# Two tokens side by side in place of four in the operands of the gate products

## The chip, the cores and the metric

The kernel runs on one core of a Trainium2 chip. The metric is the device time of one execution in microseconds (us). Before the change it is 4701.33 us, the median of 3 runs (4699.65 to 4709.9).

## What is computed

Two trunk layers on 256 context tokens and 512 latent tokens of width 1024. Each layer has a mixer (layer 0: RWKV-7 heads and a Fourier transform, layer 1: attention and a convolution) and then a PEER block, a feed-forward of 16384 small experts. The change is in PEER alone:

```python
q = (tc @ pq).reshape(PEER_CHUNK, PK_HEADS, 2, PK_HALF)
s1 = einsum("thd,hnd->thn", q[:, :, 0], sk1); s2 = einsum("thd,hnd->thn", q[:, :, 1], sk2)
v1, i1 = top_k(s1, 16);  v2, i2 = top_k(s2, 16)
score, ci = top_k(v1[..., :, None] + v2[..., None, :], 16)    # of 256 pairs
e1, e2 = i1[ci // 16], i2[ci % 16]                            # each 0 to 127
expert = e1 * 128 + e2;  gate = softmax(score)
act = gelu(einsum("thkd,td->thk", pu[expert], tc)) * gate
out = einsum("thk,thkd->td", act, pv[expert])
```

So each token has 8 heads x 16 = 128 slots, each with an expert (e1, e2) and a gate.

## The kernel before

PEER comes in two ways. For most tokens (tiles of 128: four tiles in layer 0, three in layer 1) it is computed densely: all 16384 experts are multiplied with all tokens, and the product is weighted with a gate that is zero for the experts that a token hasn't chosen. For the other tiles (two of the context in layer 0, one in layer 1) the experts' rows are gathered from DRAM, one slot at a time (`gather`): POOL issues an indirect DMA, DVE works on the 128 x 1024 row that came.

`peer` has two parts. In the first, `select` (DVE) forms e1, e2 and the gates of a tile, `dense_gates` makes of them the dense gates and writes them to DRAM (`gd`), and beside that the first NB blocks of 128 experts (60 in layer 0, 48 in layer 1) go through `up_part`: load a block of pu (SP), split it in a high and a low part (`whi` on ACT, line 378, `wlo` on DVE, line 381), 24 float32r matmuls (line 391), Gelu on ACT. In the second part the gates come back (`gt`), are multiplied with the activations, and the product with pv is summed (line 1287; for the fourth tile of layer 0 line 1316), with the remaining blocks' `up_part` in between. The gathers' steps are spread over both parts.

`dense_gates` works for a tile of 128 tokens in 32 groups of four tokens. Slots lie on the partitions: e1, e2 and the gate are transposed on PE to 128 slots x 128 tokens and written as fp16 to `ee` (gxe: e1, e2) and `gg` (gxg: the gate times 32768 as a high part and a rest). Then for each group:

- DVE, line 1106: `o` (tile o12) = one-hot codes of e1 and of e2: for each slot, 2 x 128 keys x 4 tokens, by comparison of the constant `iob` (0 to 127, each repeated for the tokens side by side) with the repeated e1 and e2.
- DVE, line 1108: `og` = the code of e1 times the gate's high part, and times its rest.
- PE, line 1114: for each token two matmuls 128 x 128 x 128 (high part, rest) into `gps`: the code of e2 is loaded as weights, `og` streams. The sum over the slots is the token's gate for each pair of e2 and e1.
- ACT, line 1116: two operations take `gps` to `gbig`, which goes to DRAM after 64 tokens.

GW is the number of tokens side by side, that is, the innermost extent of `o`, `og` and `iob`. With 4, the operands of one token's matmul are fp16 elements at a step of 4, 8 bytes.

The order of instructions on each engine is fixed when the program is built, by a scheduler; on the chip each engine goes through its queue in that order and waits on semaphores. `o` and `og` have four buffers each (OB), `gps` three.

Of the kernel before, what the change touches and what calls it, by code (L numbers as in the profile page):

```python
# [8 lines left out]
F32 = mybir.dt.float32  # L9
F32R = mybir.dt.float32r  # L10
BF16 = mybir.dt.bfloat16
F16 = mybir.dt.float16
# [3 lines left out]
OP = mybir.AluOpType  # L16
# [14 lines left out]
CQ = 3  # L31
FB = 2
GSC = 32768.0
GW = 4
GQ = 0
NO = 0
NK = 0
# [29 lines left out]
OB = 4  # L67
# [126 lines left out]
class Net:  # L194
# [26 lines left out]
    def setup(self, st):  # L221
# [22 lines left out]
        self.ka1 = ka  # L244
        self.iob = p.tile([128, 128, GW], F16, name="iob")
        nc.vector.tensor_copy(self.iob, self.k("iota")[:, :, None].to_broadcast([128, 128, GW]))
        self.io16 = p.tile([128, 16, 16], BF16, name="io16")
# [839 lines left out]
    def dense_gates(self, e1, e2, gate, gd, sp, gp, pp, pt):  # L1087

        nc = self.nc
        V = nc.vector  # L1090


        ee, gg = sp.tile([128, 2, 128], F16, name="gxe"), sp.tile([128, 2, 128], F16, name="gxg")
        for dst, x, sc in ((ee[:, 0], e1, 1.0), (ee[:, 1], e2, 1.0), (gg[:, 0], gate, GSC)):
            p = pt.tile([128, 128], F32, name="gtp")
            nc.tensor.transpose(p, x.rearrange("p a b -> p (a b)"), self.k("ident"))
            nc.scalar.mul(out=dst, in_=p, mul=sc)
        V.scalar_tensor_tensor(out=gg[:, 1], in0=p, scalar=GSC, in1=gg[:, 0], op0=OP.mult, op1=OP.subtract)
        W, H = GW, 64
        for h0 in range(0, 128, H):  # L1100
            gh = [gp.tile([128, 64, H], F32, name="gbig") for _ in range(2)]
            for t0 in range(h0, h0 + H, W):
                w = slice(t0, t0 + W)
                o = sp.tile([128, 2, 128, W], F16, name="o12", bufs=OB)
                og = sp.tile([128, 2, 128, W], F16, name="og", bufs=OB)
                V.tensor_tensor(out=o, in0=self.iob[:, None].to_broadcast([128, 2, 128, W]),  # L1106
                                in1=ee[:, :, None, w].to_broadcast([128, 2, 128, W]), op=OP.is_equal)
                V.tensor_tensor(out=og, in0=o[:, 0:1].to_broadcast([128, 2, 128, W]),  # L1108
                                in1=gg[:, :, None, w].to_broadcast([128, 2, 128, W]), op=OP.mult)
                for k0 in range(0, W, 4):  # L1110
                    p = pp.tile([128, 4, 128], F32, name="gps")
                    for j in range(4):
                        for i in range(2):
                            nc.tensor.matmul(p[:, j, :], o[:, 1, :, k0 + j], og[:, i, :, k0 + j], start=(i == 0), stop=(i == 1))  # L1114
                    for i, g in enumerate(gh):
                        nc.scalar.mul(out=g[:, :, t0 - h0 + k0:t0 - h0 + k0 + 4].rearrange("p e t -> p t e"), in_=p[:, :, i * 64:i * 64 + 64],  # L1116
                                      mul=1.0 / GSC)
            for i, g in enumerate(gh):
                nc.scalar.dma_start(gd[h0 // H, :, i * 64:i * 64 + 64, :], g)

# [500 lines left out]
```

## Time and profile before

| | |
|---|---|
| median of 3 runs | 4701.33 us (4699.65 to 4709.9) |
| the profiled execution | 4686.23 us |
| its span | 4684.4 us |
| PE, DVE, ACT, POOL busy | 91%, 76%, 37%, 34% of the span |
| PE's granted clock, mean | 0.95 |
| the gate products (line 1114) | 1792 loads and 1792 matmuls |
| the DVE operations before them (lines 1106, 1108) | 224 each |

The profile is of one execution. PE is the matmul engine, PEld its loading of weights, which can run beside a matmul; L1114 is line 1114 of the kernel before. A matmul's duration contains the time that it takes to run through the array, and matmuls overlap; what one costs in a row of them is the distance from start to start. A row of a timeline gives start, duration, engine, line, operation, output<-inputs, sizes and count. A row of windows gives a stretch, its length, then for each engine its busy time and number of instructions, then the granted clock of PE, the busy share of the DMA engines and GB/s.

### The profile page before, as it was taken

Reading aid. Unit: us, or ns where it says so; the run is one execution under the profiler, and the core shown is the slowest. Engines: PE = TensorE matmul, PEld = TensorE weight load, DVE = VectorE, ACT = ScalarE, POOL = GpSimd, SP = SyncE. Lnnn points to the kernel's source line nnn. Section 1 sums busy time; section 2 is a strip of 40 time slices with the busy share of each in tenths; the row PEclk is TensorE's granted clock in tenths of the full one; section 3 lists DMA queues with packets and bytes.
Section 4 is the critical chain, followed back from the end, with each engine's and each line's share of the span. In section 5 each row is a group of like instructions: output and inputs, shape, how many; then the busy total and the mean of one; then the engine's idle time right before and its main releaser. Section 6 shows DMA issues by size and latency. Waiting matters only on the chain. (4 is left out here: it accounts for less than half of the span.)

```text
span 4684.4 us, 69766 instructions
## 1 busy us (share of the span) xinstructions
PE 4278.9 (91%) x26113; PEld 3540.5 (76%) x26113; DVE 3552.1 (76%) x6647; ACT 1739.0 (37%) x2845; POOL 1577.4 (34%) x1146
## 2 busy tenths in 40 slices
PE   7998899985769999999999999879999989999998
PEld 5775567874647887877777888666789978888887
DVE  2776566689899887888788787695488877788885
ACT  3443123333224556222222222336436643333333
POOL 1332112214643120444444344383220024444440
PEclk9998898997889999999999999889999989999999
DMA  4444873335777767989888888410135589999994
GB/s 167 97 105 106 268 272 115 111 127 184 225 240 266 250 242 263 321 303 322 292 306 314 302 307 286 154 31 32 70 110 183 201 326 330 337 350 334 335 332 153
DMA packets 487278, 1061.99 MB, mean 227 GB/s; under 512 B 95094, under 2 KB 265846, under 8 KB 477206
## 3 DMA queue, kind: packets, MB, share of 16 engines
q1 hardware_dynamic: 371740, 594.02, 38.5%
q0 software_dynamic: 110592, 402.70, 24.6%
q10 hardware_dynamic: 4608, 60.82, 3.3%
q8 instruction: 205, 3.36, 0.3%
q14 instruction: 133, 1.09, 0.1%
HBM read 927.83 MB, written 129.56 MB: 226 GB/s over the span
## 5 line engine op out<-in xcount | busy, mean ns | idle before, releaser
L1128 POOL DMA_INDIRECT row<-in_l_pv_dram,gi x384 | 539.0, 1404 | 912.1 <-DVE rows L1142 778.1
L1128 POOL DMA_INDIRECT row<-in_l_pur_dram,gi x384 | 477.5, 1243 | 972.2 <-DVE ga L1133 511.7
L391 PE MATMUL pS<-h2hi,whi 128*128 128x512 f32 (+1 forms) x2048 | 754.6, 368 | 36.9 <-ACT a L1233 32.2
L391 PE MATMUL pS<-h2hi,wlo 128*128 128x512 f32 (+1 forms) x2048 | 752.7, 368 | 5.1 <-DVE wlo L381 5.1
L391 PE MATMUL pS<-h2lo,whi 128*128 128x512 f32 (+1 forms) x2048 | 751.8, 367 | 0.0
L1133 DVE CUSTOM_DVE_ANT_0 row<-row,rows 128x1024 f32<-128x1024 f32 x384 | 495.7, 1297 | 170.5 <-DMA row<-in_l_pur_dram,gi 168.1
L378 ACT CAST whi<-wraw 128x1024 fp32r<-128x1024 f32 x327 | 343.9, 1053 | 750.5 <-PE pS L391 571.6
L1142 DVE SCALAR_TENSOR_TENSOR rows<-row,ga,rows 128x1024 f32<-128x1024 f32 x381 | 488.2, 1281 | 158.5 <-DMA row<-in_l_pv_dram,gi 156.4
L1287 PE MATMUL acc<-vhi,ahi 128*128 128x512 f32 x1536 | 469.6, 392 | 11.3 <-ACT ahi L378 11.3
L1287 PE MATMUL acc<-vlo,ahi 128*128 128x512 f32 x1536 | 478.3, 391 | 0.0
L1287 PE MATMUL acc<-vhi,alo 128*128 128x512 f32 x1536 | 472.1, 391 | 3.5 <-DVE alo L381 3.5
L391 PEld LDWEIGHTS pS<-h2hi,whi 128*128 128x128 f32 x2048 | 390.3, 191 | 84.6 <-ACT a L1233 34.1
L391 PEld LDWEIGHTS pS<-h2hi,wlo 128*128 128x128 f32 x2048 | 389.3, 190 | 47.8 <-DVE wlo L381 6.8
L391 PEld LDWEIGHTS pS<-h2lo,whi 128*128 128x128 f32 x2048 | 390.5, 191 | 44.0
L381 DVE TENSOR_TENSOR wlo<-wraw,whi 128x1024 fp32r<-128x1024 f32 x266 | 325.6, 1224 | 85.6 <-ACT whi L378 84.8
L378 ACT CAST vhi<-vraw 128x1024 fp32r<-128x1024 f32 x256 | 265.0, 1050 | 215.3 <-PE acc L1287 107.7
L381 DVE TENSOR_TENSOR vlo<-vraw,vhi 128x1024 fp32r<-128x1024 f32 x256 | 309.8, 1221 | 40.1 <-ACT vhi L378 39.9
L1287 PEld LDWEIGHTS acc<-vhi,alo 128*128 128x128 f32 x1536 | 289.0, 188 | 66.3 <-DVE alo L381 5.1
L1287 PEld LDWEIGHTS acc<-vhi,ahi 128*128 128x128 f32 x1536 | 288.1, 189 | 65.9 <-ACT ahi L378 11.9
L1287 PEld LDWEIGHTS acc<-vlo,ahi 128*128 128x128 f32 x1536 | 289.3, 188 | 61.3
L378 ACT CAST ahi<-a32f 128x384 fp32r<-128x384 f32 (+1 forms) x148 | 83.3, 563 | 594.6 <-DVE a32f L1303 279.5
L1116 ACT ACTIVATE gbig<-gps 128x256 f32<-128x256 f32 x448 | 235.5, 661 | 156.8 <-PE gps L1114 144.4
(460 smaller groups left out, 8175.9 us busy)
## 6 DMA issues: line engine op xcount, KB each, us to landing
wraw<-in_l_pu_dram SPq DMA_DIRECT2D x256, 512.0 KB
vraw<-in_l_pv_dram SPq DMA_DIRECT2D x256, 512.0 KB
gd<-gbig ACTq DMA_DIRECT2D x28, 2048.0 KB
mw<-in_l_mod_w_dram SPq DMA_DIRECT2D x48, 1024.0 KB
gt<-gd SPq DMA_DIRECT2D x64, 512.0 KB
wraw<-in_l_pq_dram SPq DMA_DIRECT2D x48, 512.0 KB
gt<-gd SPq DMA_DIRECT2D x64, 384.0 KB
ab<-arb SPq DMA_DIRECT2D x24, 768.0 KB
```

The costliest lines, as they stand in the source:

```text
L378: e.copy(out=hi, in_=src)
L381: return (e_lo or nc.vector).tensor_tensor(out=lo, in0=src, in1=hi.bitcast(F32), op=OP.subtract)
L391: nc.tensor.matmul(ps, a[:, k, :], b[:, k, t0:t0 + n], start=s, stop=e)
L1116: nc.scalar.mul(out=g[:, :, t0 - h0 + k0:t0 - h0 + k0 + 4].rearrange("p e t -> p t e"), in_=p[:, :, i * 64:i * 64 + 64], mul=1.0 / GSC)
L1128: nc.gpsimd.indirect_dma_start(out=r, out_offset=None, in_=self.I[f"l{l}_{src}"], in_offset=bass.IndirectOffsetOnAxis(ap=idx[:, s:s + 1], ...
L1133: V.tensor_tensor_reduce(out=r, in0=r, in1=acc, scale=1.0, scalar=0.0, op0=OP.mult, op1=OP.add, accum_out=act[:, s:s + 1])
L1142: V.scalar_tensor_tensor(out=acc, in0=r, scalar=act[:, s:s + 1], in1=acc, op0=OP.mult, op1=OP.add)
L1287: nc.tensor.matmul(acc[t][h2], x[:, q], y[:, h2 * 512:(h2 + 1) * 512], start=s, stop=z)
```

## The change

GW becomes 2. `o` and `og` still hold four tokens, now as two pairs: the innermost extent is 2, and the pair's number lies outside the keys. In the same way `ee` and `gg` are held in pairs of tokens. So

- a matmul's operands, weights and stream, are fp16 elements at a step of 2, 4 bytes, in place of 4, 8 bytes;
- the two DVE operations have the same number, size and output; the operand that is repeated over the keys (`ee`, `gg`) is read in rows of 2 elements in place of 4;
- the three ACT operations and one DVE operation of a tile that fill `ee` and `gg` go in pairs of elements, and `iob` has 256 in place of 512 columns.

The program has the same instructions in the same order on every engine.

```diff
--- before.py
+++ after.py
@@ -31,7 +31,7 @@
 CQ = 3
 FB = 2
 GSC = 32768.0
-GW = 4
+GW = 2
 GQ = 0
 NO = 0
 NK = 0
@@ -1090,31 +1090,33 @@
         V = nc.vector
 
 
-        ee, gg = sp.tile([128, 2, 128], F16, name="gxe"), sp.tile([128, 2, 128], F16, name="gxg")
-        for dst, x, sc in ((ee[:, 0], e1, 1.0), (ee[:, 1], e2, 1.0), (gg[:, 0], gate, GSC)):
+        W, H = GW, 64
+        two = lambda x: x.rearrange("p (a b) -> p a b", b=W)
+        ee, gg = sp.tile([128, 64, 2, W], F16, name="gxe"), sp.tile([128, 64, 2, W], F16, name="gxg")
+        for dst, x, sc in ((ee[:, :, 0], e1, 1.0), (ee[:, :, 1], e2, 1.0), (gg[:, :, 0], gate, GSC)):
             p = pt.tile([128, 128], F32, name="gtp")
             nc.tensor.transpose(p, x.rearrange("p a b -> p (a b)"), self.k("ident"))
-            nc.scalar.mul(out=dst, in_=p, mul=sc)
-        V.scalar_tensor_tensor(out=gg[:, 1], in0=p, scalar=GSC, in1=gg[:, 0], op0=OP.mult, op1=OP.subtract)
-        W, H = GW, 64
+            nc.scalar.mul(out=dst, in_=two(p), mul=sc)
+        V.scalar_tensor_tensor(out=gg[:, :, 1], in0=two(p), scalar=GSC, in1=gg[:, :, 0], op0=OP.mult, op1=OP.subtract)
         for h0 in range(0, 128, H):
             gh = [gp.tile([128, 64, H], F32, name="gbig") for _ in range(2)]
-            for t0 in range(h0, h0 + H, W):
-                w = slice(t0, t0 + W)
-                o = sp.tile([128, 2, 128, W], F16, name="o12", bufs=OB)
-                og = sp.tile([128, 2, 128, W], F16, name="og", bufs=OB)
-                V.tensor_tensor(out=o, in0=self.iob[:, None].to_broadcast([128, 2, 128, W]),
-                                in1=ee[:, :, None, w].to_broadcast([128, 2, 128, W]), op=OP.is_equal)
-                V.tensor_tensor(out=og, in0=o[:, 0:1].to_broadcast([128, 2, 128, W]),
-                                in1=gg[:, :, None, w].to_broadcast([128, 2, 128, W]), op=OP.mult)
-                for k0 in range(0, W, 4):
-                    p = pp.tile([128, 4, 128], F32, name="gps")
-                    for j in range(4):
-                        for i in range(2):
-                            nc.tensor.matmul(p[:, j, :], o[:, 1, :, k0 + j], og[:, i, :, k0 + j], start=(i == 0), stop=(i == 1))
-                    for i, g in enumerate(gh):
-                        nc.scalar.mul(out=g[:, :, t0 - h0 + k0:t0 - h0 + k0 + 4].rearrange("p e t -> p t e"), in_=p[:, :, i * 64:i * 64 + 64],
-                                      mul=1.0 / GSC)
+            for t0 in range(h0, h0 + H, 4):
+
+                w = slice(t0 // W, t0 // W + 2)
+                o = sp.tile([128, 2, 2, 128, W], F16, name="o12", bufs=OB)
+                og = sp.tile([128, 2, 2, 128, W], F16, name="og", bufs=OB)
+                B4, B5 = [128, 4, 128, W], [128, 2, 2, 128, W]
+                V.tensor_tensor(out=o.rearrange("p a h e b -> p (a h) e b"), in0=self.iob[:, None].to_broadcast(B4),
+                                in1=ee[:, w].rearrange("p a h b -> p (a h) b")[:, :, None].to_broadcast(B4), op=OP.is_equal)
+                V.tensor_tensor(out=og, in0=o[:, :, 0:1].to_broadcast(B5), in1=gg[:, w, :, None].to_broadcast(B5), op=OP.mult)
+                p = pp.tile([128, 4, 128], F32, name="gps")
+                for j in range(4):
+                    a, b = divmod(j, W)
+                    for i in range(2):
+                        nc.tensor.matmul(p[:, j, :], o[:, a, 1, :, b], og[:, a, i, :, b], start=(i == 0), stop=(i == 1))
+                for i, g in enumerate(gh):
+                    nc.scalar.mul(out=g[:, :, t0 - h0:t0 - h0 + 4].rearrange("p e t -> p t e"), in_=p[:, :, i * 64:i * 64 + 64],
+                                  mul=1.0 / GSC)
             for i, g in enumerate(gh):
                 nc.scalar.dma_start(gd[h0 // H, :, i * 64:i * 64 + 64, :], g)
```

## Rows read from the trace of the kernel before

**Rows 1.** The profile's page, first part: busy time of the engines.
```profile
PE 4278.9 (91%) x26113; PEld 3540.5 (76%) x26113; DVE 3552.1 (76%) x6647; ACT 1739.0 (37%) x2845; POOL 1577.4 (34%) x1146
```

**Rows 2.** Windows: stretch, length, then PE, PEld, DVE, ACT, POOL, clock, DMA.
```profile
1484.00:1800.00 316.00, 316.00 (x1752) 265.20 (x1751) 268.11 (x508) 176.80 (x293) 57.54 (x41) 1.00 0.69 243
1800.00:1860.00 60.00, 52.00 (x344) 43.45 (x343) 42.06 (x66) 40.84 (x76) 0.00 (x0) 0.83 0.63 248
3520.00:3760.00 240.00, 238.09 (x1569) 229.49 (x1568) 201.03 (x447) 154.10 (x258) 0.00 (x0) 1.00 0.52 188
3760.00:3800.00 40.00, 35.56 (x234) 33.03 (x233) 29.71 (x47) 24.09 (x44) 9.54 (x8) 0.79 0.89 341
3900.00:4600.00 700.00, 698.09 (x3413) 620.00 (x3412) 560.13 (x692) 248.37 (x338) 302.82 (x220) 1.00 0.94 333
2000.00:3000.00 1000.00, 946.60 (x4093) 767.17 (x4092) 791.22 (x982) 267.18 (x360) 405.79 (x310) 0.99 0.86 295
```

**Rows 3.** Timeline of PE: float32r matmuls one behind the other, 512 and 256 columns.
```profile
1610.77 0.39 PE L391 MATMUL pS<-h2hi,whi 128*128 128x512 f32 x1
...
1614.19 0.39 PE L391 MATMUL pS<-h2hi,whi 128*128 128x512 f32 x1
...
1040.72 0.28 PE L391 MATMUL po<-hchi,whi 128*128 128x256 f32 x1
...
1041.90 0.28 PE L391 MATMUL po<-hclo,whi 128*128 128x256 f32 x1
```

**Rows 4.** Timeline of PE and PEld: a run of 24 gate pairs.
```profile
1607.44 2.73 PEld L1114 LDWEIGHTS <-o 128*128 128x128 f16 x24 [0.26 <-DVE rows L1142]
1607.45 3.02 PE L1114 MATMUL gps<-og,o 128*128 128x128 f16 x24
```

**Rows 5.** Groups by shape: busy us, mean ns of one, idle time before.
```profile
L1114 PE MATMUL gps<-og,o 128*128 128x128 f16 x1792 | 234.3, 296 | 10.8 <-ACT gbig L1116 6.2 <-DVE og L1108 3.0
...
L391 PEld LDWEIGHTS pS<-h2lo,whi 128*128 128x128 f32 x2048 | 390.5, 191 | 44.0
...
L1114 PEld LDWEIGHTS <-o 128*128 128x128 f16 x1792 | 194.1, 118 | 41.5 <-issue 21.7 <-PE gps L1114 8.7 <-DVE og L1108 2.9
...
L857 PEld LDWEIGHTS sm<-sv,M 32*32 32x32 f32 x576 | 34.0, 106 | 14.6 <-DVE sv L858 4.5 <-issue 2.1 <-DVE am L803 1.9
```

**Rows 6.** Windows, line 1114 alone: stretch, length, PE, PEld, clock, DMA.
```profile
1484.00:1800.00 316.00, 98.13 (x752) 81.37 (x753) 1.00 0.69 243
1800.00:1860.00 60.00, 35.26 (x274) 29.87 (x272) 0.83 0.63 248
3520.00:3760.00 240.00, 82.10 (x624) 67.11 (x624) 1.00 0.52 188
3760.00:3800.00 40.00, 18.85 (x144) 15.74 (x144) 0.79 0.89 341
```

**Rows 7.** Windows, line 391 alone, first main part.
```profile
1484.00:1800.00 316.00, 239.41 (x991) 182.78 (x989) 1.00 0.69 243
```

**Rows 8.** Groups of DVE by shape: busy us, mean ns; and L1077: minimum/median/maximum ns.
```profile
L1106 DVE TENSOR_TENSOR o<-iob,gxe 128x1024 f16<-128x1024 f16 x224 | 151.9, 687 | 54.0 <-PE gps L1114 52.3 <-issue 0.7 <-ACT gxe L1097 0.3
L1108 DVE TENSOR_TENSOR og<-o,gxg 128x1024 f16<-128x1024 f16 x224 | 148.1, 683 | 0.1
L381 DVE TENSOR_TENSOR wlo<-wraw,whi 128x1024 fp32r<-128x1024 f32 x266 | 325.6, 1224 | 85.6 <-ACT whi L378 84.8
...
L1077 DVE TENSOR_TENSOR teq<-taf,io x10: 1211/1220/2308, 1081.2 to 3726.4; 128x2048 bf16<-128x2048 bf16 x10
```

**Rows 9.** Waits from 1484 to 1800 us: us in total, times, longest.
```profile
POOL row L1128 <- DVE rows L1142: 152.8, 25, 9.0
...
ACT whi L378 <- PE pS L391: 43.5, 24, 3.9
...
DVE wlo L381 <- ACT whi L378: 22.6, 22, 2.6
DVE o L1106 <- PE gps L1114: 21.9, 29, 2.8
```

## The prediction, made before the run

> **What bounds the kernel now.** I began with the page's busy shares: PE is busy 91% of the span [rows 1]. A busy PE is not yet a full one, so I then read the two stretches in which the changed lines run, by windows. They lie in the first half of each PEER layer: 1484 to 1860 us and 3520 to 3800 us. In both, the main part comes first and a tail follows.
>
> In the main part of the first one (316 us) PE is busy for all of it, in that of the second for 238.1 of 240 us [rows 2]. Whether that is full is told by counting. A matmul of 512 columns in the neighbouring product (line 391) follows the last one after 0.228 us: 15 steps take 1614.19 - 1610.77 = 3.42 us [rows 3]. A gate matmul follows the last one after (3.02 - 0.296) / 23 = 0.118 us, in a run of 24 [rows 4]; the 0.296 us is the last one's own duration [rows 5]. In 316 us there are 991 of line 391 and 752 of the gate products [rows 6, 7]: 991 x 0.228 + 752 x 0.118 = 314.7 us. So PE does nothing else and hardly waits. What these 752 pairs (a load and a matmul each) cost is on the path in full. The same holds for the 624 pairs of the second main part.
>
> In the tails (274 and 144 pairs) it is otherwise: PE is busy 52.0 of 60 and 35.6 of 40 us, at a granted clock of 0.83 and 0.79 [rows 2]. For each four tokens DVE needs two operations of 0.685 us [rows 8], 1.37 us, against 8 x 0.118 = 0.94 us on PE. There DVE paces.
>
> DVE is the next engine in the main parts: 268.1 of 316 and 201.0 of 240 us [rows 2]. Its waits there are PE's doing: 21.9 us for the one-hot tile that PE still reads, and 22.6 us for ACT's whi, which itself waited 43.5 us for PE [rows 9]. Together 44.5 of its 47.9 us of idle time.
>
> **The change part by part.** No instruction comes, goes or moves on any engine; only how operands lie. So the sum has durations alone in it.
>
> 1. *The gate pairs on PE.* Load and matmul read fp16 elements 4 bytes apart in place of 8. No row has a 16-bit operand that lies closer, so the new time is bounded. From above: 0.118 us, no change. More than that I exclude, since each instruction reads the same elements from half the stretch. From below: the float32r matmuls of 256 columns, whose operands are contiguous, follow each other after 1.18 / 10 = 0.118 us [rows 3], those of 512 after 0.228; that is 0.43 ns a column, and 0.064 us at 128 columns, if the load hides behind the matmul as it does there.
>
> Does it hide here? A float32 load of 32 columns lasts 106 ns and one of 128 columns 191 ns [rows 5]: 78 ns fixed and 0.885 ns a column. The fp16 load lasts 118 ns, so some 40 ns of reading. In the run of 24, the loads stand end to end: 24 of 118 ns fill 2.73 us [rows 4, 5], one load for each step of a matmul. I read that as load and stream in turn: 40 ns, then 78 ns for 128 columns, 0.61 ns a column against the 0.43 above. Both are then slower than they need be. With the stream at 0.43 x 128 = 55 ns and the load as short as the shortest full one in these rows, 28 ns (0.885 x 32), a pair takes 83 ns. I take 84 ns: 34 ns less. It stands between the ends of 64 and 118, somewhat nearer to the first.
>
> The Trainium skill ("TensorE: Matmul & The Clock Gate", section "Back-to-back issue gap") gives some 81 ns a matmul for a steady stream of loads and matmuls at 128 columns; no run here shows it for 16 bits. An estimate by that figure is 37 ns x 1376 = 51 us of PE time in the main parts.
>
> On the path: 752 x 34 = 25.6 us and 624 x 34 = 21.2 us. PE's need falls to 290 and 219 us, DVE's stays at 268 and 201, 92% of each. The queues are served in order, so some of the idle time that DVE keeps will fall where PE needs its result; I count nine tenths, 42 us. In the tails 418 x 34 = 14 us of PE work lies beside DVE; I take 3 us of it, for the matmuls that DVE waits for there. Sum 45 us.
>
> 2. *The two DVE operations*, 224 of each, 1024 fp16 elements. The operand that is repeated now has rows of two elements in place of four. From below: 0.685 us as now. The bf16 comparison of 2048 elements in rows of 16 (line 1077) takes 1.22 us [rows 8], that is, 0.52 ns more for each further element, so rows of 4 and of 16 run at one rate. From above: the float32 operation of 1024 elements, 1.224 us [rows 8], if the chip can no longer take elements in pairs. I take the first: it is the same instruction, and two is still a pair. Nothing hides a loss here beyond DVE's idle time.
>
> 3. *The rest.* Each dense tile has three ACT operations and one of DVE on 128 x 128 that now write or read pairs: 28 instructions in all, beside PE's full work in the main parts. The constant iob has half the size. Nothing; without that cover it would be the difference of 28 short instructions.
>
> What follows a stretch is moved forward as a whole. The gathers' steps stand between the other instructions, and in the main part POOL's fetches wait for DVE (152.8 us) [rows 9], so they move with it. From 3900 to 4600 us PE is busy 698.1 of 700 us [rows 2], so layer 1's gain reaches the end; in layer 0 PE is at 946.6 of 1000 us after the stretch, with the same work behind the same work. The stretch would ask for DMA at 0.69 x 316 / 290 = 0.75 of the engines' time, while 3900 to 4600 runs at 0.94 with PE full [rows 2].
>
> The profiled execution took 4686.2 us for a span of 4684.4 us; the median of three runs is 4701.3, 15.1 us above it. 4686.2 - 45 = 4641, and with the 15.1 us 4656 us.
>
> **Rivals.**
>
> *The step does not matter (no change).* What makes 118 ns may be the turn-taking of load and matmul, not the reading: the load's 118 ns equals the spacing, and its first 78 ns are no reading at all by the fit above. Then the pair stays at 118 ns and the time at 4701 us. Against it: loads of float32 last 191 ns while their matmuls follow after 118, so a load's whole duration need not be waited for [rows 3, 5]. The Trainium skill ("Advanced Engine Details and Errata", section "Memory Cachelines") speaks for this rival: SBUF is read in lines of 16 bytes, and two accesses to one line are said to be enough for full speed. A step of 8 bytes already makes two. The trace leaves that open: the 0.61 ns a column speak against it, but they rest on my split of the 118 ns.
>
> *Only the load gains.* 40 to 28 ns, 12 x 1376 = 16.5 us on the path, 4685 us. For it: the fp16 load is longer than that of 32 columns by just this much. Against: the 23 ns that the stream has over the float32r slope would be unexplained.
>
> *DVE loses its pairs (slower).* Each of the 448 operations takes 1.224 us, 0.54 more. Layer 0: 256 x 0.54 = 138 us against 65.8 us of DVE idle time in main part and tail; layer 1: 192 x 0.54 = 104 against 49.3 us. DVE becomes the bound and the gain on PE is worth nothing: 72 + 54 = 126 us, 4827 us. It decides from about 0.94 us an operation, where the 65.8 us are used up (65.8 / 256 = 0.26 above 0.685). For it: rows this short stand nowhere in the trace. Against: rate independent of row length at 4 and 16.
>
> *A pair at the lower bound.* 64 ns, 54 x 1376 = 74 us of PE; PE's need is then 275 and 206 us, DVE 97% busy, so I count three quarters, 56 us, and 4 in the tails: 4641 us. This is the forecast's own lower half.
>
> **How the numbers follow.** Forecast, a pair between 64 and 95 ns: 0.63, time 4656 us, its own range 4636 to 4675. Load alone: 0.12. No change: 0.15. DVE slower: 0.10. What can be told from no change is 0.2%, 9.4 us. Faster: 0.63 + 0.12 = 0.75; within: 0.15; slower: 0.10. Downwards the full 74 us without loss would give 4627. The range goes from 4630 to 4706: it takes in no change with the scatter of the runs, and leaves out the slower rival and the last of the lower end.
>
> **What would show it.** In the profile after, the gate matmuls in a run should follow each other after about 84 ns, with loads of some 106 ns. L1106's and L1108's successors should still take 0.685 us; 1.2 us would be the slower rival. DVE's wait for the gate tiles (21.9 us) should shrink to a few us, and PE should show first idle time before gate loads, waiting for DVE. The two stretches should be 25 and 20 us shorter and all else as long as before. If pairs are at 84 ns and the stretches are not shorter, the step that failed is that PE bounds them; if pairs stay at 118, it is the reading.

## The result, and the profile after

The changed kernel takes 4617.97 us (median of 4 runs, 4613.54 to 4629.15) against 4700.49 us of the kernel before (4 runs, 4692.45 to 4709.9): ratio 0.9827 [0.9802, 0.9853], 82.5 us less. The same pair was run again later: 4616.06 against 4696.14 us, ratio 0.9821 [0.9799, 0.9842], 80.1 us less. Forecast were 4656 us and a range of 4630 to 4706. So the direction was right, and the gain of 45 us was a little over half of the real one; the time lies below the range.

The profiled execution of the changed kernel took 4615.68 us (span 4613.9 us). In the changed kernel the lines named before are shifted: L1106 is L1109, L1108 is L1111, L1114 is L1116, L1116 is L1118, L1128 is L1130, L1142 is L1144. So L1116 below is the gate matmul where a row is of the changed kernel, and the ACT operation behind it where a row is of the kernel before.

What answers to [rows 4]: a run of 24 gate pairs on PE, from the timeline of after (start us, length us, engine, line, operation, output<-inputs, sizes, count).

```profile
1490.33 1.38 PEld L1116 LDWEIGHTS <-o 128*128 128x128 f16 x24 [0.26 <-issue]
1490.33 1.55 PE L1116 MATMUL gps<-og,o 128*128 128x128 f16 x24
...
1549.48 1.55 PE L1116 MATMUL gps<-og,o 128*128 128x128 f16 x24
```

The length without the last matmul's own 0.218 us, over 23 steps, is the distance from start to start: (1.55 - 0.218) / 23 = 58 ns. It was 118 ns, and 84 ns were forecast. It is also less than the 64 ns that the prediction held for the lower bound.

The groups by shape of after, to be read beside [rows 5] and [rows 8] (busy us, mean ns of one, idle time before and what ended it):

```profile
L1116 PE MATMUL gps<-og,o 128*128 128x128 f16 x1792 | 137.5, 229 | 20.2 <-DVE og L1111 10.9 <-ACT gbig L1118 9.3
...
L1116 PEld LDWEIGHTS <-o 128*128 128x128 f16 x1792 | 113.0, 102 | 48.1 <-issue 26.6 <-PE gps L1116 12.8 <-DVE og L1111 2.4
...
L1109 DVE TENSOR_TENSOR o<-iob,gxe 128x1024 f16<-128x1024 f16 x224 | 149.0, 686 | 13.7 <-PE gps L1116 13.5
L1111 DVE TENSOR_TENSOR og<-o,gxg 128x1024 f16<-128x1024 f16 x224 | 148.4, 686 | 0.1
```

The two DVE operations take 686 ns as before. DVE's idle time ahead of the first of them, for the gate tiles that PE had not finished, fell from 52.3 us [rows 8] to 13.5 us. PE now has 10.9 us of idle time before gate matmuls that wait for DVE; it was 3.0 us [rows 5].

Windows of after, to be read beside [rows 2] (stretch, length, PE, PEld, DVE, ACT, POOL, clock, DMA). The main part of layer 0, its tail, the main part of layer 1, its tail:

```profile
1484.00:1762.00 278.00, 278.00 (x1782) 227.37 (x1781) 264.92 (x511) 177.71 (x298) 81.04 (x41) 1.00 0.77 274
1762.00:1815.00 53.00, 39.62 (x315) 32.09 (x315) 40.21 (x64) 37.97 (x73) 0.00 (x0) 0.77 0.67 268
3482.00:3700.00 218.00, 214.75 (x1643) 206.64 (x1642) 204.92 (x458) 156.56 (x267) 0.00 (x0) 0.98 0.60 219
3700.00:3725.00 25.00, 16.47 (x135) 14.97 (x133) 18.60 (x32) 17.16 (x33) 7.49 (x7) 0.73 0.98 363
```

And the two parts of PE's work in the first of these stretches, line 1116 alone and line 391 alone, as [rows 6] and [rows 7]:

```profile
1484.00:1762.00 278.00, 53.91 (x768) 44.58 (x768) 1.00 0.77 274
...
1484.00:1762.00 278.00, 242.89 (x1005) 184.17 (x1004) 1.00 0.77 274
```

1005 x 0.228 + 768 x 0.058 = 273.7 of 278 us. PE is still full in the main part, though DVE beside it is now busy 264.9 of 278 us (95%). By counting, 4.3 us of the 278 are left over, against 1.3 of 316 us before. In the tails PE is busy for a smaller share of the time (75% of 53 us where it was 87% of 60, and 66% of 25 where it was 89% of 40 us), and DVE for the same share or a larger one (76% where it was 70%, and 74% as before).

Where the time came from is seen at the first and last run of gate pairs of each layer. Timeline of PE, kernel before:

```profile
1488.12 2.98 PE L1114 MATMUL gps<-og,o 128*128 128x128 f16 x24
...
1845.06 4.45 PE L1114 MATMUL gps<-og,o 128*128 128x128 f16 x32
...
3532.61 3.00 PE L1114 MATMUL gps<-og,o 128*128 128x128 f16 x24
...
3788.76 1.11 PE L1114 MATMUL gps<-og,o 128*128 128x128 f16 x8 [0.65 <-DVE og L1108]
```

The same of after, whose first run stands above (1490.33):

```profile
1804.57 1.86 PE L1116 MATMUL gps<-og,o 128*128 128x128 f16 x16 [0.20 <-DVE og L1111]
...
3494.52 1.55 PE L1116 MATMUL gps<-og,o 128*128 128x128 f16 x24
...
3718.47 1.01 PE L1116 MATMUL gps<-og,o 128*128 128x128 f16 x8 [0.74 <-DVE og L1111]
```

From the start of the first run to the end of the last, with the same 2042 and 1680 matmuls of PE between them in both kernels: in layer 0 361.4 us before and 316.1 us after (45.3 less), in layer 1 257.3 and 225.0 us (32.3 less). Together 77.6 us. The whole profiled executions differ by 70.5 us: in that of after the first gate pair starts 2.2 us later, 5.0 us more lie between the two stretches (1688.1 against 1683.1 us), and what follows the last pair is as long as before (894.4 and 894.5 us). So nothing was gained outside the stretches, and the 7 us lost there are less than the distance between executions of one kernel (4692.45 to 4709.9 us before). The medians lie 80 to 82 us apart, more than these two executions, because the one of before is 14 us under its median and the one of after 2 us.

The last run of layer 0 in after has 16 pairs at (1.86 - 0.308) / 15 = 103 ns, where 0.308 us is a matmul's own duration there: from 1804.5 to 1806.5 us the granted clock is 0.50, the lower of its two levels (1.2 GHz), behind a tail in which PE idles for a quarter of the time. In the tails, where DVE paces, the shorter pair is partly given back in this way.

### The profile page after: what moved, and what is told of

The parts are those of the page before. It is cut to its first block, busy times and chain, and to the rows that moved or that the text cites. A ratio compares the mean times of both kernels' runs of the same rounds, so it can differ in the third digit from the quotient of the medians.

```text
span 4613.9 us, 69765 instructions
## 1 busy us (share of the span) xinstructions
PE 4200.0 (91%) x26113; PEld 3460.6 (75%) x26113; DVE 3543.7 (77%) x6647; ACT 1734.0 (38%) x2845; POOL 1602.3 (35%) x1146
## 5 line engine op out<-in xcount | busy, mean ns | idle before, releaser
L1130 POOL DMA_INDIRECT row<-in_l_pv_dram,gi x384 | 562.9, 1466 | 846.3 <-DVE rows L1144 701.1
L1130 POOL DMA_INDIRECT row<-in_l_pur_dram,gi x384 | 478.1, 1245 | 944.6 <-DVE ga L1135 515.7
L1144 DVE SCALAR_TENSOR_TENSOR rows<-row,ga,rows 128x1024 f32<-128x1024 f32 x381 | 488.5, 1282 | 159.3 <-DMA row<-in_l_pv_dram,gi 157.2
L391 PEld LDWEIGHTS pS<-h2hi,whi 128*128 128x128 f32 x2048 | 390.2, 191 | 84.7 <-ACT a L1235 33.7
L1118 ACT ACTIVATE gbig<-gps 128x256 f32<-128x256 f32 x448 | 232.4, 669 | 111.3 <-PE gps L1116 95.0
```

The lines of the kernel that those rows point to most:

```text
L391: nc.tensor.matmul(ps, a[:, k, :], b[:, k, t0:t0 + n], start=s, stop=e)
L1118: nc.scalar.mul(out=g[:, :, t0 - h0:t0 - h0 + 4].rearrange("p e t -> p t e"), in_=p[:, :, i * 64:i * 64 + 64], mul=1.0 / GSC)
L1130: nc.gpsimd.indirect_dma_start(out=r, out_offset=None, in_=self.I[f"l{l}_{src}"], in_offset=bass.IndirectOffsetOnAxis(ap=idx[:, s:s + 1], ...
L1144: V.scalar_tensor_tensor(out=acc, in0=r, scalar=act[:, s:s + 1], in1=acc, op0=OP.mult, op1=OP.add)
```

## The experiments

Three theories stood after the result. Theory 1: the step of the streamed operand (`og`) alone sets the pair's time. Theory 2: the step of the weights (`o`) sets it. Theory 3, the prediction's own: load and stream stand in turn, so each contributes its part. A fourth question was whether anything but PE gains from the new layout.

The six kernels that stand beside after in the table are the changed kernel with another view of the same tiles in the matmul of line 1116. They read elements of other tokens, so the gates are wrong; instructions, their order and all other operands are those of after. "Pair" is the distance from start to start in a run of 24, as above; the granted clock is 1.00 in each of these runs. Each ratio is against executions of the kernel before that were taken beside that kernel (medians 4695 to 4702 us).

| kernel | step of weights, stream (elements) | pair, ns | median us (runs) | against before |
|---|---|---|---|---|
| both1 | 1, 1 | 56 | 4609.91 (4) | 0.9815 [0.9785, 0.9844] |
| after | 2, 2 | 58 | 4617.97 (4) | 0.9827 [0.9802, 0.9853] |
| load4 | 4, 2 | 60 | 4626.87 (4) | 0.9829 [0.98, 0.9858] |
| stream3 | 2, 3 | 87 | 4681.35 (1) | one run |
| stream4 | 2, 4 | 116 | 4701.14 (10) | 1.0004 [0.9987, 1.0021] |
| both4 | 4, 4 | 118 | 4694.22 (10) | 0.9997 [0.9983, 1.0011] |
| stream8 | 2, 8 | 228 | 4953.98 (1) | one run |

### load4: the weights alone at the old step

```diff
-nc.tensor.matmul(p[:, j, :], o[:, a, 1, :, b], og[:, a, i, :, b], start=(i == 0), stop=(i == 1))
+nc.tensor.matmul(p[:, j, :], o.rearrange("p a h e b -> p (a h e b)")[:, 512:512 + 512].rearrange("p (e x) -> p e x", x=4)[:, :, j % 4], og[:, a, i, :, b], start=(i == 0), stop=(i == 1))
```

> The changed kernel, but the weights of each gate matmul are read at a step of 4 elements (8 bytes) again, from the same one-hot tile; the stream keeps its step of 2. What is read is not the right token's code. Theory 1 (the stream's step sets a pair's time): pairs stay at 58 ns, time as changed, 4618 us. Theory 2 (the load's step sets it): 118 ns, time as before, 4700 us. Theory 3 (load and stream in turn, each slowed by its own step, as the prediction read it): the pair in between, 70 to 95 ns, 4640 to 4670 us.

Measured: the gain stays whole, 4626.87 us. The run of 24 in load4, then its loads: the group, and their minimum/median/maximum in ns with the first and last start in us.

```profile
1572.21 1.61 PE L1116 MATMUL gps<-og,o 128*128 128x128 f16 x24
```

```profile
L1116 PEld LDWEIGHTS <-o 128*128 128x128 f16 x1792 | 119.3, 118 | 48.6 <-issue 25.6 <-PE gps L1116 13.1 <-DVE og L1111 2.1
```

```profile
L1116 PEld LDWEIGHTS <-o x1792: 110/113/149, 1511.9 to 3749.6; 128*128 128x128 f16 x200
```

The loads last 118 ns in the mean, as long as before the change, and a pair follows the last one after (1.61 - 0.221) / 23 = 60 ns. So the loads lie over each other, and half of a load's duration is simply not waited for. Theories 2 and 3 fall here. The median is 9 us above that of after; the interval holds that of after, and the profiled run lost 21.6 of its 34.0 us over the profiled run of after ahead of the first gate pair (1511.9 us in place of 1490.3), where no gate pair stands.

### stream4: the streamed operand alone at the old step

```diff
-nc.tensor.matmul(p[:, j, :], o[:, a, 1, :, b], og[:, a, i, :, b], start=(i == 0), stop=(i == 1))
+nc.tensor.matmul(p[:, j, :], o[:, a, 1, :, b], og.rearrange("p a h e b -> p (a h e b)")[:, 512 * i:512 * i + 512].rearrange("p (e x) -> p e x", x=4)[:, :, j % 4], start=(i == 0), stop=(i == 1))
```

> The changed kernel, but the streamed operand of each gate matmul is read at a step of 4 elements (8 bytes) again; the weights keep their step of 2. What is streamed is not the right token's. Theory 1 (stream): 118 ns a pair, 4700 us. Theory 2 (load): 58 ns, 4618 us. Theory 3 (in turn): 80 to 105 ns, 4650 to 4680 us.

Measured: the whole gain is gone, 4701.14 us, ratio 1.0004. The run of 24 and the groups of stream4:

```profile
1561.68 2.67 PEld L1116 LDWEIGHTS <-o 128*128 128x128 f16 x24 [0.26 <-issue]
1561.69 2.96 PE L1116 MATMUL gps<-og,o 128*128 128x128 f16 x24
```

```profile
L1116 PE MATMUL gps<-og,o 128*128 128x128 f16 x1792 | 231.1, 295 | 11.1 <-ACT gbig L1118 6.2 <-DVE og L1111 3.0
L1116 PEld LDWEIGHTS <-o 128*128 128x128 f16 x1792 | 192.4, 115 | 40.2 <-issue 22.7 <-PE gps L1116 9.1 <-DVE og L1111 2.5
```

(2.96 - 0.295) / 23 = 116 ns. The loads read the same weights as in after, where they last 102 ns, and last 115 ns here: a load's row also depends on the matmul that it stands beside, though not in step with it (101 ns in stream3, 118 ns in stream8). Theory 1 holds.

### both4: both at the old step, all else in the new layout

```diff
-nc.tensor.matmul(p[:, j, :], o[:, a, 1, :, b], og[:, a, i, :, b], start=(i == 0), stop=(i == 1))
+nc.tensor.matmul(p[:, j, :], o.rearrange("p a h e b -> p (a h e b)")[:, 512:512 + 512].rearrange("p (e x) -> p e x", x=4)[:, :, j % 4], og.rearrange("p a h e b -> p (a h e b)")[:, 512 * i:512 * i + 512].rearrange("p (e x) -> p e x", x=4)[:, :, j % 4], start=(i == 0), stop=(i == 1))
```

> The changed kernel with DVE's and ACT's new layout, but both operands of the gate matmuls read at a step of 4 elements. What is read is not the right token's. If the step alone makes the gain: 118 ns a pair, 4700 us, as before the change. If the layout on DVE and ACT, or the placing in SBUF, has a part in it: the time lies below 4690 us with pairs at 118 ns.

Measured: 4694.22 us, ratio 0.9997 [0.9983, 1.0011]. The run of 24:

```profile
1558.23 3.00 PE L1116 MATMUL gps<-og,o 128*128 128x128 f16 x24
```

(3.00 - 0.297) / 23 = 118 ns a pair. Written pairs on ACT, shorter rows on DVE and the smaller constant are worth nothing that can be told; part 3 of the prediction ("Nothing") was right.

### both1: contiguous operands

```diff
-nc.tensor.matmul(p[:, j, :], o[:, a, 1, :, b], og[:, a, i, :, b], start=(i == 0), stop=(i == 1))
+nc.tensor.matmul(p[:, j, :], o.rearrange("p a h e b -> p (a h e b)")[:, 128 * j:128 * j + 128], og.rearrange("p a h e b -> p (a h e b)")[:, 256 * j + 128 * i:256 * j + 128 * i + 128], start=(i == 0), stop=(i == 1))
```

> The changed kernel, but both operands of the gate matmuls are read without a gap (step of 1, 2 bytes). What is read is not the right token's. If a step of 2 still costs something, pairs fall below 58 ns and the time below 4612 us; if 128 columns at the granted clock are the bound (128 / 2.4 = 53 ns, and the 4 to 5 ns that a float32r matmul has beyond its columns or less), pairs stay at 57 to 58 ns and the time at 4618 us.

```profile
1550.66 1.51 PE L1116 MATMUL gps<-og,o 128*128 128x128 f16 x24
```

(1.51 - 0.217) / 23 = 56 ns, 2 ns less than in after. So at a step of two the stream has hardly anything more to give: at the granted clock of 1.00 (2.4 GHz), an estimate of one column a cycle makes 53 ns for 128 columns. The median, 4609.91 us, lies 8 us below that of after, and the intervals overlap widely; 2 ns on each of 1792 pairs would be 3.6 us. The expectation's "4 to 5 ns" of a float32r matmul beyond its columns does not come out of [rows 3], where it is 118 - 107 = 11 and 228 - 213 = 15 ns; 58 - 53 = 5 ns is what a pair of after has.

### stream3 and stream8: the size of the effect

```diff
-nc.tensor.matmul(p[:, j, :], o[:, a, 1, :, b], og[:, a, i, :, b], start=(i == 0), stop=(i == 1))
+nc.tensor.matmul(p[:, j, :], o[:, a, 1, :, b], og.rearrange("p a h e b -> p (a h e b)")[:, 384 * i:384 * i + 384].rearrange("p (e x) -> p e x", x=3)[:, :, j % 3], start=(i == 0), stop=(i == 1))
```

> The changed kernel, but the streamed operand of each gate matmul is read at a step of 3 elements (6 bytes); the weights keep their step of 2. What is streamed is not the right token's. So far a pair takes 56 ns at a step of 1, 58 at 2 and 117 at 4. If the time goes with the bytes that the 128 columns span (768 against 1024): about 88 ns. If a step beyond 4 bytes halves the rate at once: 117 ns. If up to three quarters of the span are free: 58 ns.

```diff
-nc.tensor.matmul(p[:, j, :], o[:, a, 1, :, b], og[:, a, i, :, b], start=(i == 0), stop=(i == 1))
+nc.tensor.matmul(p[:, j, :], o[:, a, 1, :, b], og.rearrange("p a h e b -> p (a h e b)")[:, 0:0 + 1024].rearrange("p (e x) -> p e x", x=8)[:, :, j % 8], start=(i == 0), stop=(i == 1))
```

> The changed kernel, but the streamed operand of each gate matmul is read at a step of 8 elements (16 bytes); the weights keep their step of 2. What is streamed is not the right token's. If the time goes with the bytes spanned: about 234 ns a pair, twice that at a step of 4, and a time near 4800 us or above. If beyond a step of 4 bytes each element costs the same, whatever the distance: 117 ns and 4700 us.

The runs of 24 in stream3, then in stream8:

```profile
1575.53 2.25 PE L1116 MATMUL gps<-og,o 128*128 128x128 f16 x24
```

```profile
1589.33 5.65 PE L1116 MATMUL gps<-og,o 128*128 128x128 f16 x24
```

(2.25 - 0.254) / 23 = 87 ns at a step of 3 and (5.65 - 0.408) / 23 = 228 ns at 8. From 2 to 8 the pair's time goes straight with the step: 58, 87, 116, 228 ns, 28 to 29 ns for each further element. In bytes that a row of 128 columns spans: 512 / 58, 768 / 87, 1024 / 116 and 2048 / 228 are all 8.8 to 9.0 bytes a ns. No step beyond 16 bytes was run, so whether the cost goes on growing with the distance is not shown.

### gw1: one token side by side

Here every gate is made from its own token's elements again. Rows of the repeated operand on DVE have one element.

```diff
-GW = 2
+GW = 1
...
-        ee, gg = sp.tile([128, 64, 2, W], F16, name="gxe"), sp.tile([128, 64, 2, W], F16, name="gxg")
+        ee, gg = sp.tile([128, 128 // W, 2, W], F16, name="gxe"), sp.tile([128, 128 // W, 2, W], F16, name="gxg")
```

> The changed kernel with GW = 1: no two tokens side by side, so matmul operands lie without a gap, and the operand that DVE repeats over the keys has rows of one element. The result is computed in full. If DVE takes fp16 elements in pairs only where a row has two of them (the slower rival's condition): the two operations take 1.22 us in place of 0.686, 448 x 0.54 = 242 us more DVE work against some 90 us that DVE is idle in the two stretches: 4618 + 120 to 180 us, and PE waits for DVE. If the row's length doesn't matter to DVE: 0.686 us as now, pairs at 56 ns, and a time of about 4612 us.

Measured: 4822.1 us (2 runs, 4810.43 and 4833.77), ratio 1.0256 [1.0214, 1.0297]. The groups of gw1, and a run of 24:

```profile
L1111 DVE TENSOR_TENSOR og<-o,gxg 128x1024 f16<-128x1024 f16 x224 | 267.7, 1233 | 0.0
L1109 DVE TENSOR_TENSOR o<-iob,gxe 128x1024 f16<-128x1024 f16 x224 | 267.2, 1231 | 2.4 <-ACT gxe L1099 1.5 <-PE gps L1116 0.9
L1116 PE MATMUL gps<-og,o 128*128 128x128 f16 x1792 | 178.2, 264 | 175.1 <-DVE og L1111 166.4 <-ACT gbig L1118 3.6 <-DVE tz L1055 0.3
```

```profile
1576.69 1.51 PE L1116 MATMUL gps<-og,o 128*128 128x128 f16 x24
```

DVE takes 1.23 us an operation, and PE, with pairs of 56 ns in its runs, as in both1, waits 166.4 us for it. The order of the instructions is not quite that of after here. This is the prediction's slower rival, at a row length of one: it was priced at 1.224 us and 4827 us. At a row length of two it does not happen.

### nb64, nb68: does the freed time in the tail have a use?

After the change PE is busy 39.6 of 53 us in the first tail. So more blocks of `up_part` were moved from the second part of PEER into the first, where they can lie beside the gates. Both compute the whole result.

```diff
-PACE = [(60, 0.5, 0.25, 3), (48, 0.5, 0.5, 3)]
+PACE = [(64, 0.5, 0.25, 3), (52, 0.5, 0.5, 3)]
```

> The changed kernel with 64 and 52 blocks of experts in the first part of the PEER layers in place of 60 and 48. The result is computed in full. If DVE paces the tail of the gate products and PE idles there (some 20 to 35 us in layer 0, 10 to 20 in layer 1), 4 more blocks of 5.4 and 4.2 us fill idle time and the second part has as much less to do: 10 to 30 us less than the changed kernel, 4590 to 4608 us. If the scheduler's order, the extra DMAs of the stored activations or DVE's own work eat it: 4615 to 4640 us.

4606.98 us (4 runs, 4597.3 to 4638.1), ratio 0.982 [0.9778, 0.9862]. It was run again together with the changed kernel itself and a step further:

> The changed kernel once more, beside the two below on one chip, for comparison with them: 4618 us, 0.982 to 0.984 of the kernel before.

> 64 and 52 blocks in the first part once more. If its 4607 us were more than chance: 8 to 15 us below the changed kernel on the same chip, since PE's idle time in the tail of layer 0 was filled. If not: within 5 us of it.

```diff
-PACE = [(60, 0.5, 0.25, 3), (48, 0.5, 0.5, 3)]
+PACE = [(68, 0.5, 0.25, 3), (54, 0.5, 0.5, 3)]
```

> 68 and 54 blocks in the first part; the result is computed in full. If PE's idle time in the tails is still not used up with 64 and 52: another 3 to 10 us less than with 64 and 52. If it is used up, or if the tail's gates come later and the second part waits for them: no gain, up to 10 us more.

After_again 4616.06 us (5 runs, 4601.5 to 4621.25), ratio 0.9821 [0.9799, 0.9842]; nb64_again 4606.91 (5 runs, 4594.33 to 4619.91), 0.9813 [0.979, 0.9837]; nb68 4629.28 (5 runs, 4616.43 to 4639.93), 0.9862 [0.9838, 0.9886]. 64 and 52 blocks came out 9 to 11 us below the changed kernel both times, but the intervals overlap widely: a gain of this size is likely and not shown. 68 and 54 came out 13 us above the changed kernel (the two intervals just overlap), though the tail is filled. The row that tells that is layer 1's tail, in after and then in nb68:

```profile
3700.00:3730.00 30.00, 21.47 (x164) 19.97 (x162) 21.88 (x35) 19.19 (x36) 9.16 (x8) 0.77 0.98 372
```

```profile
3700.00:3730.00 30.00, 30.00 (x241) 28.82 (x240) 25.31 (x39) 19.43 (x36) 3.66 (x3) 1.00 0.73 264
```

PE is full to the end of the stretch in nb68, but the last gate pair starts at 3747.9 us in place of 3719.2, and the wait that the gates end in stands behind it as before: once, PE waits 14.6 us for the first high part (`ahi`) of the gated activations, 11.4 us in after (us, times, longest; after, then nb68):

```profile
PE acc L1289 <- ACT ahi L378: 11.4, 1, 11.4
```

```profile
PE acc L1289 <- ACT ahi L378: 14.6, 1, 14.6
```

The blocks moved forward didn't take the place of that wait; whether this explains all of the 13 us between the medians was not settled.

## Why the prediction came out as it did

**PE bounds the two stretches: right.** The stretches got shorter by 45.3 and 32.3 us, and the rest of the program moved as a whole, to within 7 us. With the pairs at half their time PE is still full in the main part of layer 0.

**The gate pairs: the direction right, the size wrong. This is the step that failed.** The prediction split the 118 ns of a pair: "I read that as load and stream in turn: 40 ns, then 78 ns for 128 columns". Stream4 and load4 show that the 118 ns were the stream alone, at a step of 8 bytes, and that the load lay beside it at next to no cost (2 ns a pair). The split's fixed part and slope, 78 ns and 0.885 ns a column, are durations of loads, and a load's duration is not what is waited for. The evidence for the split was that the loads stood end to end at 118 ns each [rows 4, 5] (24 of 118 ns would fill 2.83 us and not the 2.73 us of the row, yet but for the first two they do stand end to end). But when the pairs are 60 ns apart, loads of 113 ns (the median in that run) lie over each other (load4), so the equality said nothing. The rule that the prediction had for float32r, a paragraph earlier ("if the load hides behind the matmul as it does there"), held for fp16 as well; its numbers, loads of 191 ns beside matmuls that follow after 118 ns, had been used against a rival only. The loads of 191 ns in [rows 5] belong to matmuls of 512 and 384 columns; those of the matmuls that follow after 118 ns last as long, as two of them show, in the run of 256 columns of [rows 3]:

```profile
1041.43 0.19 PEld L391 LDWEIGHTS po<-hclo,whi 128*128 128x128 f32 x1
...
1041.55 0.19 PEld L391 LDWEIGHTS po<-hchi,wlo 128*128 128x128 f32 x1
```

The sign "loads of some 106 ns" nearly came (102 ns in the mean) and says nothing for the split. The prediction's other estimate, 81 ns a pair, was too long in the same way: 58 ns were measured.

**The lower bound was no bound.** The 64 ns took in the fixed part of the slope from float32r matmuls of 512 and 256 columns; at 128 columns of fp16 a pair takes 58 ns, and 56 with contiguous operands. 0.43 ns a column alone, 55 ns, would have been the bound.

**What lies on the path: right, as a fraction.** The prediction counted nine tenths of the pairs' gain in the main parts and 3 us in the tails. With the measured 60 ns in place of 34: 1376 x 60 = 82.6 us, nine tenths are 74.3, and with the 3 us 77.3 us; the two stretches gave 77.6. So the pair's time is enough to explain the miss. That the sums agree to 0.3 us is partly luck: nine tenths of the main parts' pairs are 40.6 and 33.7 us, and the layers gave 45.3 and 32.3. The reason given for the tenth did not show either, as PE hardly waited for DVE in the main parts. Of the 107.5 us that 60 ns make on all 1792 pairs, some 30 did not come; 10.7 us of these are idle time of PE in the two stretches, which grew from 12.7 to 23.5 us, and the lower clock in the tails has a part in the rest that was not measured. The rival "a pair at the lower bound" had the mechanism, but counted only three quarters of the gain, for a DVE at 97%: with DVE busy for 95% of the main part, PE shows no idle time there (278.00 of 278 us).

**DVE: right.** 686 ns at rows of two, as taken, and gw1 shows that the upper end (1.224 us) was the right price for the case that didn't come, one row length further.

**The rival "the step does not matter": disproved.** Twice the bytes between elements cost twice the time, stream4 against after. The Trainium skill ("Advanced Engine Details and Errata", section "Memory Cachelines") asks for at least two accesses to a line of 16 bytes, which the prediction took to be enough for full speed; for the streamed operand of a matmul these runs do not agree: a step of 8 bytes, two elements in 16 bytes, runs at half the rate of a step of 4 (116 against 58 ns). The measurement decides.

**The waits: mostly right.** The waits of after from 1484 to 1762 us (us in total, times, longest), against [rows 9]:

```profile
POOL row L1130 <- DVE rows L1144: 112.1, 26, 7.7
ACT gbig L1118 <- PE gps L1116: 58.9, 35, 4.2
...
ACT whi L378 <- PE pS L391: 31.6, 16, 3.9
...
DVE wlo L381 <- ACT whi L378: 9.3, 9, 4.9
...
DVE o L1109 <- PE gps L1116: 1.5, 3, 0.5
```

DVE's wait for the gate tiles shrank from 21.9 to 1.5 us, as forecast. Idle time of PE for DVE came too (10.9 us before gate matmuls in the groups of after), but hardly in the main part.

## What to carry to other kernels

Read a row of matmuls from start to start and divide by columns: where that is far above what contiguous operands take in the same trace (0.43 ns a column here), look first at the step of the streamed operand and not at the load, whose duration may be hidden almost in full. It is worth time only where PE is what the stretch waits for. Lay out what is streamed so that neighbouring columns are at most 4 bytes apart, and let the weights have the larger step if one of the two must. The layout is bounded from the other side by the engine that writes it: two 16-bit elements side by side kept VectorE at 0.686 us, with one it took 1.23 us.

## What the runs showed of the hardware

- A load and a matmul of 128 x 128 x 128 in fp16 follow the last ones after 56, 58, 87, 116 and 228 ns where the streamed elements are 2, 4, 6, 8 and 16 bytes apart, at a granted clock of 1.00. An estimate from these: 4 bytes of the spanned stretch for each cycle of 2.4 GHz (53, 80, 107, 213 ns for steps of 4 to 16 bytes), and 5 to 15 ns more for each pair. Whether it goes by bytes or by elements, only the float32r matmuls bear on: contiguous, 4 bytes apart, 0.43 ns a column [rows 3], as fp16 at a step of 4 bytes (58 / 128 = 0.45).
- A step of 8 in place of 4 bytes in the weights costs 2 ns a pair at most (58 to 60, 116 to 118 ns), though a load's row grows from 102 to 118 ns (after and load4).
- A DVE operation on 1024 fp16 elements with a repeated operand takes 0.686 us where that operand's rows have two elements and 1.23 us where they have one.
